# Input laid out transposed as well, norm factor applied at eviction, attention steps moved off VectorE, row work of the end spread

## Chip, cores, metric

One core of a Trainium2 chip runs the whole layer in one launch. The metric is device time in microseconds; the median of three runs of the kernel before is 1140.7 us (1139.41 to 1140.78).

## The reference

One decoder layer on 1024 rows of 1024 columns in float32, with sandwich norms:

```
n    = rmsnorm(x) * pre_mix_gain
proj = n @ w_in                       # u | v | q | k | value | forget logits
a_u, a_v = gelu(proj_u), gelu(proj_v)
a    = a_u * (tril(w_spatial) @ layernorm(a_v) + b_spatial)      # 128-row chunks, 8 groups
logf = log_sigmoid(proj_f + b_f);  c = cumsum(logf)
b    = softmax(q k^T / 8 + c_q - c_k, causal) @ value             # 8 heads of 64, blocks of 128 queries
mix  = [rmsnorm(a) | rmsnorm(b)] @ w_out
h    = x + rmsnorm(mix)
ff   = (silu(n2 @ w_gate) * (n2 @ w_up)) @ w_ffn_out,  n2 = rmsnorm(h)
out  = h + rmsnorm(ff)
```

The norm of x is a factor per row (the reciprocal root of the row's mean square) times a gain per column. A factor per row commutes with the product by w_in; a gain per column does not.

## The kernel before

Every product is made of three products of fp32r halves: `split` (line 113) copies a tile to its high part on ScalarE and subtracts that on VectorE (or GpSimd) for the low part; `mm3` (118) issues high x high, high x low and low x high on TensorE. Loads and stores are all issued on SP's queue, which is in order. The tile framework orders the instructions of each engine by program order and by readiness in its own model, and sets the semaphores; the order on each engine is then fixed.

Stage by stage:

- **Front, value and forget columns ("bv").** For each of 8 row tiles, `norm_load` reads x, `norm_scale` (185 to 190) takes the square sum on ScalarE, the root on VectorE and GpSimd (`rstd`) and multiplies by root and gain on VectorE, and `norm_tr` transposes 8 blocks of 128x128 on TensorE and splits them from PSUM into `nth`/`ntl`, which stay for all projections. Then 48 products of 256 and 264 columns per tile; `split` evicts them into `vs`, and the forget logits go to `fz`. The weights come in 4 pairs of pieces through three `stage` buffers.
- **"av" and "au"**: the same with 512 columns, GELU on ScalarE, layer norm, spatial gating; cumulative sums of the log gates are transposed and stored to `c_d`.
- **Attention**, 4 pairs of heads. `qk_steps` makes q and k transposed, evicting with the factor -1/8 (442 to 449); for pairs 2 to 4 its products are pumped in between the blocks of the pair before. For 64 blocks (head, 128 queries): `prep` on GpSimd, `scores` on TensorE, a fused add-and-minimum on VectorE, the exponential with its sum on ScalarE, a reciprocal of the sum on VectorE (499), `probs` (transposes and splits), `values` every second block, whose result is copied out of PSUM by VectorE (543), and `finish`. `qu_load` (461) brings a unit's queries by four DMAs into one of three buffers. In the last pair w_out is loaded and the first two row tiles are merged.
- **Mix, feed-forward up, feed-forward down**, in Strassen-like forms of seven products. The down projection runs the products 1, 2, 6, 5, 7, 3, 4 with 11 steps each; every step is 12 products of 512 columns, and its operands are loaded and split four steps ahead. In product 4 the row work runs beside: steps 0 to 3 do `square` for both halves of one tile each (multiplication by the gain on GpSimd) and `ffn_tail` (root, two fused multiply-adds on VectorE, two stores); steps 3 to 6 load the h rows of the other four tiles and do their second half. The last four steps are then done tile by tile, and after each, `after` does the first half and the tail of that tile.

Of the kernel before, what the change touches and what calls it, by code (L numbers as in the profile page):

```python
# [36 lines left out]
QUB = 3  # L37
# [12 lines left out]
def hybrid_block(ctx: ExitStack, tc: tile.TileContext, io: dict, out: bass.AP):  # L50
# [40 lines left out]
    rsum = const.tile([P, NT, NH], F32, tag="rsum", name="rsum")  # L91

    an_d = dram.tile([S, AW], F32, tag="an_d", name="an_d")
    bo_d = dram.tile([S, AW], F32, tag="bo_d", name="bo_d")
    c_d = dram.tile([NH * NT, P], F32, tag="c_d", name="c_d")
# [10 lines left out]
    def rstd(ss, n, eps):  # L106
        m = small()
        nc.vector.tensor_scalar(out=m, in0=ss, scalar1=1.0 / n, scalar2=eps, op0=ALU.mult, op1=ALU.add)
        r = small()
        nc.gpsimd.tensor_tensor(out=r, in0=m, in1=mhalf, op=ALU.pow)  # L110
        return r
# [48 lines left out]
    def load_pair(src, width, name, k2, fine=False):  # L160
        raw = stage(f"raw_{name}_{k2}")[:, :2 * width].rearrange("p (a w) -> p a w", a=2)
# [15 lines left out]
    g1 = xp.tile([P, D], F32, tag="g1", name="g1")  # L177
    spare = mixd.rearrange("p t c -> p (t c)")

    def norm_load(t):  # L180
        xt = xp.tile([P, D], F32, tag="x", name=f"x_{t}", bufs=2)
        nc.sync.dma_start(out=xt, in_=x[t * P:(t + 1) * P, :])
        return xt
# [22 lines left out]
    g1_row = spare[0:1, 2 * D:3 * D]  # L206
    nc.sync.dma_start(out=g1_row, in_=io["pre_mix_gain"].rearrange("(o d) -> o d", o=1))
    xts = {0: norm_load(0)}
# [6 lines left out]
    gain = []  # L215
    for b in range(2):
        cs = slice(b * 512, b * 512 + 512)
        o = bank("S", f"g1_{b}")
        nc.tensor.matmul(o, ones[0:1, :], g1_row[:, cs], start=True, stop=True)
        gain.append((cs, o))  # L220
    norm_scale(0, xts[0], gain)
    norm_tr(0, xts[0])
    wvf = [w for k2 in range(KT // 2) for w in load_pair(io["w_bvf"], 520, "bv", k2, True)]
    for cs, o in gain:
        nc.scalar.copy(out=g1[:, cs], in_=o)
    xts[1] = norm_load(1)
    norm_scale(1, xts[1])

# [6 lines left out]
    for t in range(NT):  # L235
        if t + 2 < NT:
            xts[t + 2] = norm_load(t + 2)
        if t + 1 < NT:
            norm_tr(t + 1, xts[t + 1])
        if t + 2 < NT:  # L240
            norm_scale(t + 2, xts[t + 2])
# [7 lines left out]
        for b in range(2):  # L249
# [4 lines left out]
            split(o[:, :256].rearrange("p (h d) -> p h d", d=HD), vs[t][:, hs, :HD], vs[t][:, hs, HD:])  # L254
            if b == 1:
                nc.vector.tensor_tensor(out=fz[:, :, t], in0=o[:, 256:264], in1=bfb, op=ALU.add)
# [26 lines left out]
    def cum_sum():  # L283
# [4 lines left out]
        nc.vector.memset(ct[:, 64:128], 0.0)  # L288
# [6 lines left out]
    def c_rows():  # L295
        o = bank("O", "cT")
        nc.tensor.transpose(o[:, 0:P], ct, ident)
        nc.vector.tensor_copy(out=crow[0:64, :], in_=o[0:64, 0:P])
        nc.sync.dma_start(out=c_d, in_=crow[0:64, :])
# [27 lines left out]
    for t in range(NT):  # L327
# [9 lines left out]
        nc.scalar.activation(v, o, AF.Gelu)  # L337
# [29 lines left out]
    for t in range(NT):  # L367
# [10 lines left out]
        nc.scalar.activation(a, o, AF.Gelu)  # L378
# [31 lines left out]

    cb0 = [cb_tile(f"cb_0_{h}") for h in range(2)]
# [10 lines left out]
    def qk_steps(p):  # L422
# [7 lines left out]
        for which in range(2):  # L430
            tags = ("X", "S") if p == 0 and which == 1 else ("mm", "mm")
            oo = [bank(tags[half], f"qk_{p}_{which}_{half}") for half in range(2)]
            for k in range(KT):
                w = qw[p, which, k // 2]
                for half in range(2):
                    mm3(oo[half], w[:, 0, k % 2, :], w[:, 1, k % 2, :], nth[half][:, k, :], ntl[half][:, k, :],
                        k == 0, k == KT - 1)
                    if k == KT - 1:
                        o = oo[half]
                        ts = slice(half * 512, half * 512 + 512)  # L440
                        if which == 0:
                            qh, ql = [q[:, ts] for q in qp[p]]
                            nc.scalar.activation(qh, o, AF.Copy, scale=-0.125)
                            nc.vector.scalar_tensor_tensor(out=ql, in0=o, scalar=-0.125, in1=qh.bitcast(F32),
                                                           op0=ALU.mult, op1=ALU.subtract)
# [17 lines left out]
    class Block:  # L463
# [15 lines left out]
        def scores(self):  # L479
# [17 lines left out]
            ssum = small()  # L497
            nc.scalar.activation(sm[:, :n], sm[:, :n], AF.Exp, bias=m, scale=-1.0, accum_out=ssum)  # L498
            nc.vector.reciprocal(out=rsum[:, self.i, hh:hh + 1], in_=ssum)
# [16 lines left out]
    class Unit:  # L516
# [14 lines left out]
        def values(self):  # L531
# [11 lines left out]
            nc.vector.tensor_copy(out=self.osb, in_=o[:, :2 * P])  # L543
# [621 lines left out]
    def row_tiles(t):  # L1165
        ht = po.tile([P, D], F32, tag="ht", name=f"ht_{t}", bufs=4)
        nc.sync.dma_start(out=ht, in_=h_d[t * P:(t + 1) * P, :])
        rows[t] = ht, small(2, "sq"), po.tile([P, D], F32, tag="y", name=f"y_{t}", bufs=4)

    def square(t, dh, src, eng):  # L1170
        ht, ss, y = rows[t]
        cs = slice(dh * 512, dh * 512 + 512)
# [4 lines left out]
    def ffn_tail(t):  # L1177
        ht, ss, y = rows[t]
        ts = slice(t * P, (t + 1) * P)
        r = rstd2(ss)  # L1180
        for dh in range(2):
            cs = slice(dh * 512, dh * 512 + 512)
            nc.vector.scalar_tensor_tensor(out=ht[:, cs], in0=y[:, cs], scalar=r, in1=ht[:, cs],
                                           op0=ALU.mult, op1=ALU.add)
            nc.sync.dma_start(out=out[ts, cs], in_=ht[:, cs])
# [6 lines left out]
    def after(p, i):  # L1192
# [16 lines left out]
        else:  # L1209
            square(t1, 0, a, nc.vector)  # L1210
            ffn_tail(t1)
# [82 lines left out]
```

## Time and profile before

| what | value |
|---|---|
| median of three runs | 1140.7 us |
| profiled execution | 1140.83 us |
| its span, first to last instruction | 1138.8 us |
| VectorE, ScalarE, GpSimd busy | 722.2, 515.2, 177.7 us |
| mean granted TensorE clock | 0.993 |
| DMA | 188.29 MB, 165 GB/s on average |

The busy time of TensorE is made of matmuls whose ends are modelled, so that successive ones overlap; the distance between their starts is what one costs. Waits count where TensorE has them; those of other engines cost something only when TensorE stands because of them.

### The profile page before, as it was taken

The page shows a single profiled execution, that of the slowest core. Times are in us where ns is not written, and L with a number is a line of the kernel's source. Part 1 is how long each engine was busy: PE and PEld are TensorE (multiplying, and loading weights), DVE is VectorE, ACT ScalarE, POOL GpSimd, SP SyncE. Part 2 cuts the span into 40 slices and gives each one's busy share as a digit, 9 for nine tenths or more (in the row PEclk, how much of TensorE's full clock was granted, in tenths as well). Part 3 has the DMA queues.
Part 4 walks back from the last instruction along what each step waited for, and adds up shares of the span by engine and source line. Part 5 has one row for each costly group of instructions (what it writes and reads, how often), then busy time and mean ns, then how long its engine had stood idle before and what let it go on. Part 6 is the DMA issues. An engine that isn't in the chain of part 4 may idle for free.

```text
span 1138.8 us, 15652 instructions
## 1 busy us (share of the span) xinstructions
PE 1102.8 (97%) x5421; PEld 915.8 (80%) x5421; DVE 722.2 (63%) x1291; ACT 515.2 (45%) x994; POOL 177.7 (16%) x247
## 2 busy tenths in 40 slices
PE   8999999999999989999999999999999999999995
PEld 6988787888887867877888888888888888888883
DVE  5565423677779656789766576657665454644575
ACT  6343324566568534564333434333333435444461
POOL 3032203334438321000000000000000000200042
PEclk9999999999999999999999999999999999999997
DMA  8120214233355453557665557455744587666665
GB/s 268 58 93 2 74 48 140 77 98 91 87 137 151 133 194 109 177 201 251 230 220 187 185 185 242 165 185 185 243 163 148 211 268 249 196 191 197 193 196 186
DMA packets 86241, 188.29 MB, mean 165 GB/s; under 512 B 9937, under 2 KB 28433, under 8 KB 83474
## 3 DMA queue, kind: packets, MB, share of 16 engines
q1 hardware_dynamic: 86162, 187.29, 50.8%
q8 instruction: 43, 0.70, 0.3%
q14 instruction: 36, 0.29, 0.1%
HBM read 129.28 MB, written 49.58 MB: 157 GB/s over the span
## 4 chain that ended last, share of the span: by engine, by line
PE 54%; DVE 4%; issue 2%; DMA 2%; POOL 1%; ACT 1%; SPq 0%; DVEq 0%; POOLq 0%; ACTq 0%
PE guA L119 7%; PE guA L121 6%; PE guA L120 6%; PE guC L119 3%; PE guC L120 3%; PE guC L121 3%; PE dA L119 3%; PE dA L120 3%; PE dA L121 3%; PE dC L120 3%; PE dC L119 3%; PE dC L121 3%; PE guE L120 2%; PE guE L121 2%; PE guE L119 2%
## 5 line engine op out<-in xcount | busy, mean ns | idle before, releaser
L1175 POOL TENSOR_TENSOR y<-c,gpo 128x512 f32<-128x512 f32 x12 | 20.5, 1731 | 596.3 <-DMA dwr<-ws_d 476.7
L116 DVE TENSOR_TENSOR dal<-dar,dah 128x512 fp32r<-128x512 f32 x77 | 56.4, 734 | 86.6 <-ACT dah L115 84.6
L115 ACT CAST dah<-dar 128x512 fp32r<-128x512 f32 x77 | 48.0, 624 | 102.9 <-PE dC L120 45.8
L120 PE MATMUL dA<-dwl,dah 128*128 128x512 f32 x176 | 69.4, 394 | 3.0 <-DVE dwl L116 3.0
L119 PE MATMUL dA<-dwh,dah 128*128 128x512 f32 x176 | 69.6, 395 | 2.4 <-ACT dah L115 2.4
L121 PE MATMUL dA<-dwh,dal 128*128 128x512 f32 x176 | 69.0, 392 | 0.0
L474 POOL TENSOR_SCALAR sm<-cb,csq 128x128 f32<-128x128 f32 (+3 forms) x64 | 50.6, 791 | 89.9 <-PE pt L509 79.0
L498 ACT ACTIVATE sm<-sm,st 128x128 f32<-128x128 f32 (+3 forms) x64 | 50.0, 781 | 27.7 <-DVE st L494 27.3
L116 DVE TENSOR_TENSOR ptl<-pt,pth 128x512 fp32r<-128x512 f32 (+2 forms) x96 | 51.7, 554 | 10.4 <-ACT pth L115 9.8
L116 DVE TENSOR_TENSOR dwl<-dwr,dwh 128x512 fp32r<-128x512 f32 x77 | 55.4, 720 | 3.7 <-ACT dwh L115 3.6
L115 ACT CAST pth<-pt 128x512 fp32r<-128x512 f32 (+2 forms) x96 | 43.7, 477 | 27.4 <-PE pt L509 27.1
L119 PE MATMUL mx<-woh,mh 128*128 128x512 f32 x128 | 51.6, 403 | 2.6 <-ACT mh L115 2.6
L119 PE MATMUL qk<-nth,qkw 128*128 128x512 f32 x128 | 53.5, 419 | 0.5 <-DVE k L116 0.4
L492 PE MATMUL s<-k,qu 128*128 128x384 f32 (+4 forms) x192 | 51.0, 365 | 1.5 <-DVE st L494 1.4
L116 DVE TENSOR_TENSOR fbc_0l<-ts,fbc_0h 128x1024 fp32r<-128x1024 f32 x22 | 26.9, 1223 | 38.8 <-ACT fbc_0h L115 38.8
L121 PE MATMUL mx<-woh,ml 128*128 128x512 f32 x128 | 50.2, 395 | 1.2 <-DVE ml L116 1.2
L119 PE MATMUL dC<-dwh,dah 128*128 128x512 f32 x132 | 51.3, 389 | 0.0
L120 PE MATMUL dC<-dwl,dah 128*128 128x512 f32 x132 | 51.3, 389 | 0.0
L121 PE MATMUL dC<-dwh,dal 128*128 128x512 f32 x132 | 51.3, 389 | 0.0
L121 PE MATMUL qk<-nth,qkw 128*128 128x512 f32 x128 | 50.5, 395 | 0.1
L120 PE MATMUL qk<-ntl,qkw 128*128 128x512 f32 x128 | 50.4, 394 | 0.0
L120 PE MATMUL mx<-wol,mh 128*128 128x512 f32 x128 | 50.2, 392 | 0.0
(749 smaller groups left out, 3251.3 us busy)
## 6 DMA issues: line engine op xcount, KB each, us to landing
graw<-in_w_gu SPq DMA_DIRECT2D x21, 1024.0 KB, 5.4
wj<-in_w_ffn_out SPq DMA_DIRECT2D x22, 512.0 KB, 4.2
aj<-ff_d SPq DMA_DIRECT2D x22, 512.0 KB, 3.7
dar<-as_d SPq DMA_DIRECT2D x44, 256.0 KB, 3.6
dwr<-ws_d SPq DMA_DIRECT2D x44, 256.0 KB, 3.7
dwr<-in_w_ffn_out SPq DMA_DIRECT2D x33, 256.0 KB, 4.0
dar<-ff_d SPq DMA_DIRECT2D x33, 256.0 KB, 4.4
ff_d<-g SPq DMA_DIRECT2D x22, 256.0 KB, 5.4
```

The lines of the kernel that those rows point to most:

```text
L115: nc.scalar.copy(out=hi, in_=src)
L116: (lo_eng or nc.vector).tensor_tensor(out=lo, in0=src, in1=hi.bitcast(F32), op=ALU.subtract)
L119: nc.tensor.matmul(o, ah, bh, start=first, stop=False, **kw)
L120: nc.tensor.matmul(o, ah, bl, start=False, stop=False, **kw)
L121: nc.tensor.matmul(o, al, bh, start=False, stop=last, **kw)
L474: nc.gpsimd.tensor_scalar(out=sm[:, :n], in0=cbs[hh][:, :n], scalar1=csq[:, hh * NT + i:hh * NT + i + 1], scalar2=1.0, op0=ALU.add, op1=AL ...
L492: nc.tensor.matmul(o[:, :w], qu[:, hl, ts], ks_[hh][:, ks], start=hl == 0, stop=hl == 1)
L498: nc.scalar.activation(sm[:, :n], sm[:, :n], AF.Exp, bias=m, scale=-1.0, accum_out=ssum)
L1175: eng.tensor_tensor(out=y[:, cs], in0=src, in1=gpo[:, cs], op=ALU.mult)
```

## The change

- **Front.** The host array x is also passed as `x_t`, laid out so that a tile's load gives the transposed blocks, and the gain as a column per block. `x_split` multiplies by the gain (a column value spread over 128 rows) and splits, on VectorE and ScalarE. The transposes are gone. `x_norm` still loads x and takes the square sum; the factors go to `rst`. They are applied where products leave PSUM: in `split_scaled`, in the forget logits, as a scale of the GELUs, and for q and k by a multiplication with a row of factors (`rrow`), which is stored with the cumulative sums and loaded back to all partitions. The last pair of weight pieces has a buffer of its own.
- **Attention.** The exponential's sum goes straight into `rsum`; the reciprocal is taken once per row tile in `merge_norm`. The values' bank is copied by ScalarE. The query buffers (`QUB`) fall from 3 to 2.
- **End.** h rows are loaded and a first half done in steps 2 to 5 of product 6, a second tile's half in product 3; product 4 does the rest in steps 2 to 5, and the stores one step later. All multiplications are on VectorE. At the very end the tail of a tile comes behind the first half of the next.

```diff
-QUB = 3
+QUB = 2
...
+        raw = xp.tile([P, 1040], F32, tag="raw3", name="raw_bv_3") if (name, k2) == ("bv", 3) else stage(...)
...
-    def norm_scale(t, xt, gain=None):
-        ss = small()
-        nc.scalar.activation(spare[...], xt, AF.Square, accum_out=ss)
-        r = rstd(ss, D, RMS_EPS)
-        for cs, g in gain or [(slice(0, D), g1)]:
-            nc.vector.scalar_tensor_tensor(out=xt[:, cs], in0=xt[:, cs], scalar=r, in1=g, op0=ALU.mult, op1=ALU.mult)
-    def norm_tr(t, xt):
-        transposed(lambda k: xt[:, k * P:(k + 1) * P], nth[t // 4][:, :, tok(t)], ntl[t // 4][:, :, tok(t)], f"n{t}")
+    def x_columns(t):
+        xt = xp.tile([P, KT, P], F32, tag="xT", name=f"xT_{t}", bufs=2)
+        src = io["x_t"][t].rearrange("p (k t) -> p k t", t=P)
+        for ks in (slice(0, 4), slice(4, 8)) if t == 0 else (slice(0, 8),):
+            nc.sync.dma_start(out=xt[:, ks, :], in_=src[:, ks, :])
+        return xt
+    def x_split(t, xt, parts=1):
+        for i in range(parts):
+            ks = slice(i * KT // parts, (i + 1) * KT // parts)
+            nc.vector.tensor_tensor(out=xt[:, ks, :], in0=xt[:, ks, :],
+                                    in1=g1[:, ks].unsqueeze(2).broadcast_to([P, KT // parts, P]), op=ALU.mult)
+            split(xt[:, ks, :], nth[t // 4][:, ks, tok(t)], ntl[t // 4][:, ks, tok(t)])
+    def x_norm(t):
+        xt = xp.tile([P, D], F32, tag="x", name=f"x_{t}", bufs=2)
         nc.sync.dma_start(out=xt, in_=x[t * P:(t + 1) * P, :])
+        ss = small()
+        nc.scalar.activation(spare[...], xt, AF.Square, accum_out=ss)
+        rstd(ss, D, RMS_EPS, rst[:, t:t + 1])
+    def split_scaled(src, hi, lo, t):
+        r = rst[:, t:t + 1]
+        nc.scalar.activation(hi, src, AF.Copy, scale=r)
+        nc.vector.scalar_tensor_tensor(out=lo, in0=src, scalar=r, in1=hi.bitcast(F32), op0=ALU.mult, op1=ALU.subtract)
...
+    x_split(0, xts[0], 2)
     wvf = [w for k2 in range(KT // 2) for w in load_pair(io["w_bvf"], 520, "bv", k2, True)]
+    xts[1] = x_columns(1)
+    x_split(1, xts[1])
+    x_norm(0)
...
         if t + 2 < NT:
+            xts[t + 2] = x_columns(t + 2)
+            x_split(t + 2, xts[t + 2])
         if t + 1 < NT:
-            norm_tr(t + 1, xts[t + 1])
+            x_norm(t + 1)
...
-        nc.scalar.activation(v, o, AF.Gelu)
+        nc.scalar.activation(v, o, AF.Gelu, scale=rst[:, t:t + 1])
...
+    rrow = at.tile([P, S], F32, tag="rrow", name="rrow")
+    nc.sync.dma_start(out=rrow.rearrange("p (t n) -> p t n", n=P),
+                      in_=c_d[NH * NT:, :].rearrange("t n -> (t n)").partition_broadcast(P))
...
+                        t = stage(f"qkt_{p}_{which}_{half}")[:, :512]
+                        nc.vector.scalar_tensor_tensor(out=t, in0=o, scalar=1.0 if which else -0.125, in1=rrow[:, ts],
+                                                       op0=ALU.mult, op1=ALU.mult)
                         if which == 0:
-                            nc.scalar.activation(qh, o, AF.Copy, scale=-0.125)
-                            nc.vector.scalar_tensor_tensor(out=ql, in0=o, scalar=-0.125, ...)
+                            split(t, *[q[:, ts] for q in qp[p]])
                         else:
-                                split(o[own, :], ks_[2 * p + h][own, ts], ks_[2 * p + h][oth, ts])
+                                split(t[own, :], ks_[2 * p + h][own, ts], ks_[2 * p + h][oth, ts])
...
-            nc.scalar.activation(sm[:, :n], sm[:, :n], AF.Exp, bias=m, scale=-1.0, accum_out=ssum)
-            nc.vector.reciprocal(out=rsum[:, self.i, hh:hh + 1], in_=ssum)
+            nc.scalar.activation(sm[:, :n], sm[:, :n], AF.Exp, bias=m, scale=-1.0,
+                                 accum_out=rsum[:, self.i, hh:hh + 1])
...
-            nc.vector.tensor_copy(out=self.osb, in_=o[:, :2 * P])
+            nc.scalar.copy(out=self.osb, in_=o[:, :2 * P])
...
+        nc.vector.reciprocal(out=rsum[:, t, :], in_=rsum[:, t, :])
...
-    def square(t, dh, src, eng):
+    def square(t, dh, src, y):
...
-        eng.tensor_tensor(out=y[:, cs], in0=src, in1=gpo[:, cs], op=ALU.mult)
+        nc.vector.tensor_tensor(out=y, in0=src, in1=gpo[:, dh * 512:dh * 512 + 512], op=ALU.mult)
...
-            square(t1, 0, a, nc.vector)
-            ffn_tail(t1)
+            square(t1, 0, a, po.tile([P, 512], F32, tag="y", name=f"y_{t1}", bufs=4))
+            if i > 0:
+                ffn_tail(PAIRS[i - 1][1])
+            if i == 3:
+                ffn_tail(t1)
...
-            if p == 4 and j < 4:
-                t0, t1 = PAIRS[j]
-                for dh in range(2):
-                    square(t0, dh, parts[("c11", "c12")[dh], j], nc.gpsimd)
-                ffn_tail(t0)
-            if p == 4 and 3 <= j < 7:
-                t1 = PAIRS[j - 3][1]
-                row_tiles(t1)
-                square(t1, 1, parts["c22", j - 3], nc.gpsimd)
+            if p in (6, 3, 4) and 1 < j < 6:
+                t0, t1 = PAIRS[j - 2]
+                if p == 6:
+                    row_tiles(t0)
+                    square(t0, 0, parts["c11", j - 2], parts["c11", j - 2])
+                elif p == 3:
+                    row_tiles(t1)
+                    square(t1, 1, parts["c22", j - 2], parts["c22", j - 2])
+                else:
+                    square(t0, 1, parts["c12", j - 2], parts["c12", j - 2])
+                    ffn_tail(t0, False)
+            if p == 4 and 2 < j < 7:
+                tail_store(PAIRS[j - 3][0])
```

`ffn_tail(t, store)` leaves its two stores out when `store` is false, and `tail_store` issues them.

## Rows read from the trace of the kernel before

**Rows 1.** The page: busy us, share of the span, instructions.
```profile
PE 1102.8 (97%) x5421; PEld 915.8 (80%) x5421; DVE 722.2 (63%) x1291; ACT 515.2 (45%) x994; POOL 177.7 (16%) x247
```
**Rows 2.** Windows: stretch, then busy us of each engine, clock, DMA share, GB/s.
```profile
10.00:20.00 10.00, 8.88 (x58) 8.44 (x58) 7.00 (x10) 8.37 (x16) 5.40 (x5) 1.00 0.84 267
30.00:60.00 30.00, 30.00 (x254) 30.00 (x253) 13.72 (x29) 11.14 (x24) 1.65 (x3) 1.00 0.13 42
```
**Rows 3.** TensorE in order of time, front: start, length, line; then one tile's transposes.
```profile
9.99 0.58 PE L119 MATMUL bv<-wh_bv,nth 128*128 128x256 f32 x1 [0.46 <-ACT nth L115]
...
33.18 1.03 PE L128 MATMUL tp_n<-ident,x 128*128 128x128 f32 x8
33.97 0.36 PE L119 MATMUL bv<-wh_bv,nth 128*128 128x256 f32 x1
...
65.55 0.40 PE L119 MATMUL av<-wh_av,nth 128*128 128x512 f32 x1
...
L128 PE MATMUL tp_n<-ident,x x64: 270/272/474, 7.6 to 53.9; 128*128 128x128 f32 x64
```
**Rows 4.** ScalarE in order of time: the first square of x.
```profile
4.75 1.06 ACT L187 ACTIVATE mixd<-x 128x1024 f32<-128x1024 f32 x1 [2.69 <-DMA x<-in_x]
```
**Rows 5.** Groups by line and shape: busy us, mean ns, idle before them.
```profile
L190 DVE SCALAR_TENSOR_TENSOR x<-x,st,g 128x1024 f32<-128x1024 f32 x7 | 9.0, 1285 | 4.2 <-POOL st L110 4.2
L499 DVE RECIPROCAL rsum<-st 128x1 f32<-128x1 f32 x64 | 10.3, 161 | 20.3 <-ACT sm L498 20.1
L543 DVE COPY osb<-o 128x256 f32<-128x256 f32 x31 | 12.9, 417 | 6.0 <-PE o L541 6.0
L444 DVE SCALAR_TENSOR_TENSOR ql<-qk,qh 128x512 fp32r<-128x512 f32 x8 | 5.5, 690 | 3.6 <-ACT qh L443 3.6
L443 ACT ACTIVATE qh<-qk 128x512 fp32r<-128x512 f32 x8 | 4.8, 594 | 3.2 <-PE qk L121 3.2
L115 ACT CAST pth<-pt 128x256 fp32r<-128x256 f32 x16 | 5.9, 370 | 4.4 <-PE pt L509 4.4
```
**Rows 6.** Windows of attention: three head pairs; the start of the last.
```profile
200.00:330.00 130.00, 129.01 (x803) 111.62 (x801) 94.81 (x287) 76.64 (x196) 49.98 (x91) 1.00 0.35 95
340.00:350.00 10.00, 7.53 (x47) 5.55 (x45) 9.89 (x28) 7.80 (x20) 9.11 (x10) 1.00 0.59 164
```
**Rows 7.** The query tile: issue and landing of its loads; two blocks' scores.
```profile
L461 SPq DMA_DIRECT2D qu<-qh x64: 461/558/668, 178.4 to 364.9; - x64
DMA to landing us min/median/max: 1.9/2.0/4.9
...
337.25 1.36 PE L492 MATMUL s<-k,qu 128*128 128x384 f32 x4
342.88 0.47 PE L492 MATMUL s<-k,qu 128*128 128x448 f32 x1
```
**Rows 8.** The last stall: SP's waits for stores, TensorE, SP, two windows.
```profile
SPq L1185 <- DVE ht L1183: 24.4, 15, 10.4
...
1113.37 0.42 SPq L1100 DMA_DIRECT2D dar<-ff_d  x1
...
1115.29 0.50 PE L120 MATMUL dA<-dwl,dah 128*128 128x512 f32 x1 [2.97 <-DVE dwl L116]
1118.46 0.80 PE L119 MATMUL dA<-dwh,dah 128*128 128x512 f32 x1 [2.40 <-ACT dah L115]
...
1115.00:1120.00 5.00, 2.32 (x6) 1.52 (x7) 1.52 (x3) 0.71 (x2) 0.00 (x0) 0.58 0.90 313
1120.00:1125.00 5.00, 5.00 (x18) 4.04 (x17) 1.92 (x3) 1.96 (x5) 0.00 (x0) 0.73 0.12 48
```
**Rows 9.** After the last product: TensorE's last, then VectorE's last tile.
```profile
1129.83 0.39 PE L121 MATMUL dA<-dwh,dal 128*128 128x512 f32 x1
...
1132.87 0.68 DVE L1175 TENSOR_TENSOR y<-dA,gpo 128x512 f32<-128x512 f32 x1
...
1134.34 1.41 DVE L1183 SCALAR_TENSOR_TENSOR ht<-y,st,ht 128x512 f32<-128x512 f32 x2 [0.67 <-POOL st L103]
```

More of the change, by code (lines that the diff above doesn't have):

```diff
@@ L160, in load_pair @@
     def load_pair(src, width, name, k2, fine=False):
-        raw = stage(f"raw_{name}_{k2}")[:, :2 * width].rearrange("p (a w) -> p a w", a=2)
+        raw = xp.tile([P, 1040], F32, tag="raw3", name="raw_bv_3") if (name, k2) == ("bv", 3) else stage(f"raw_{name}_{k2}")
+        raw = raw[:, :2 * width].rearrange("p (a w) -> p a w", a=2)
         rows = src[k2 * 2 * P:(k2 + 1) * 2 * P, :].rearrange("(a p) w -> p a w", p=P)
@@ L214, in hybrid_block @@
                             compare_op=ALU.is_equal, fill=0.0)
[L215 to L222, printed above, removed]
+    x_split(0, xts[0], 2)
     wvf = [w for k2 in range(KT // 2) for w in load_pair(io["w_bvf"], 520, "bv", k2, True)]
[L224 to L227, printed above, removed]
+    xts[1] = x_columns(1)
+    x_split(1, xts[1])
+    x_norm(0)
     fz = fp.tile([P, NH, NT], F32, tag="fz", name="fz")
@@ L287, in cum_sum @@
         tot = o[:, 64:128].rearrange("p (h t) -> p h t", t=NT)
[L288 removed]
+        nc.vector.memset(ct[:, 64 + NT:128], 0.0)
+        nc.vector.tensor_copy(out=ct[:, 64:64 + NT], in_=rst)
         nc.vector.memset(car[:, :, 0], 0.0)
@@ L1165, in row_tiles, with tail_store, ffn_tail @@
     def row_tiles(t):
-        ht = po.tile([P, D], F32, tag="ht", name=f"ht_{t}", bufs=4)
+        ht = po.tile([P, D], F32, tag="ht", name=f"ht_{t}", bufs=NT)
         nc.sync.dma_start(out=ht, in_=h_d[t * P:(t + 1) * P, :])
-        rows[t] = ht, small(2, "sq"), po.tile([P, D], F32, tag="y", name=f"y_{t}", bufs=4)
-    def square(t, dh, src, eng):
-        ht, ss, y = rows[t]
-        cs = slice(dh * 512, dh * 512 + 512)
+        rows[t] = ht, po.tile([P, 2], F32, tag="ssq", name=f"ssq_{t}", bufs=NT), {}
+    def square(t, dh, src, y):
+        ht, ss, ys = rows[t]
         s = po.tile([P, 512], F32, tag="junk", name=f"junk_{t}_{dh}", bufs=2)
         nc.scalar.activation(s, src, AF.Square, scale=D ** -0.5, accum_out=ss[:, dh:dh + 1])
-        eng.tensor_tensor(out=y[:, cs], in0=src, in1=gpo[:, cs], op=ALU.mult)
-    def ffn_tail(t):
-        ht, ss, y = rows[t]
-        ts = slice(t * P, (t + 1) * P)
+        nc.vector.tensor_tensor(out=y, in0=src, in1=gpo[:, dh * 512:dh * 512 + 512], op=ALU.mult)
+        ys[dh] = y
+    def tail_store(t):
+        for dh in range(2):
+            cs = slice(dh * 512, dh * 512 + 512)
+            nc.sync.dma_start(out=out[t * P:(t + 1) * P, cs], in_=rows[t][0][:, cs])
+    def ffn_tail(t, store=True):
+        ht, ss, ys = rows[t]
         r = rstd2(ss)
@@ L1182, in ffn_tail @@
             cs = slice(dh * 512, dh * 512 + 512)
-            nc.vector.scalar_tensor_tensor(out=ht[:, cs], in0=y[:, cs], scalar=r, in1=ht[:, cs],
+            nc.vector.scalar_tensor_tensor(out=ht[:, cs], in0=ys[dh], scalar=r, in1=ht[:, cs],
                                            op0=ALU.mult, op1=ALU.add)
-            nc.sync.dma_start(out=out[ts, cs], in_=ht[:, cs])
+        if store:
+            tail_store(t)
     def down_step(o, p, j, i, fresh):
@@ L1220, in hybrid_block @@
         banks = ABANK if p in (1, 6, 7, 4) else cbank
-        if p == 4:
-            for i in range(4):
-                row_tiles(PAIRS[i][0])
         late = range(NJ - 4, NJ) if p == 4 else range(0)
@@ L1269 @@
         "x": a["x"][0],
+        "x_t": a["x"][0].reshape(NT, P, KT, P).transpose(0, 3, 2, 1).reshape(NT, P, KT * P),
+        "pre_mix_gain_t": a["pre_mix_gain"][0].reshape(KT, P).T,
         "w_au": w_in[:, 0:512],
```

36 lines of the change are left out of this document (14 added, 22 removed).

## The prediction

> **What bounds the kernel now.** I read the page first: TensorE is busy for 97% of the span and VectorE for 63% [rows 1]. A count of busy time does not say what a change is worth, so I went on to the windows and to the order of time on TensorE. Only where TensorE starts late, waits, or does something that is no product can time be won. Three places stand out. In the front, products begin at 9.99 and the first projection (the value and forget columns) lasts until 65.55 [rows 3], though TensorE is fully busy from 30 on [rows 2]: late start, waits, and transposes between the tiles. In the middle, attention leaves TensorE 1.0 us idle of 130, and then 2.5 us in the 10 us from 340, where VectorE is busy for 9.9 of 10 [rows 6]. At the end TensorE stops for 2.97 and 2.40 us, runs at a granted clock of 0.58 there, and after its last product at 1129.8 another 9 us pass until the span ends [rows 8, 9].
>
> **Front: the input comes transposed.** Removed per tile of 128 rows are 8 transposes on TensorE. In the rows they start at 33.18 and the next product at 33.97: 0.79 us. From there to 65.55 lie the products of five tiles and three more such groups, so a tile's products take (31.58 - 3 x 0.79) / 5 = 5.84 us, and its period falls from 6.63 to 5.84 [rows 3]. Six tiles in steady state give 6 x 0.79 = 4.7 us. The rest is in the start. Today TensorE waits for: the row to land (4.75), its square sum, the root, the scaling, the transposes, the split [rows 4]. After the change the root is needed only where products leave PSUM, so before the first product stand a multiplication of half a tile (half of the 1.285 us of the scaling, 0.65) and its copy (0.59 for 512 columns, as the scaled copy of the queries [rows 5]): 4.75 + 0.65 + 0.59 = 6.0, and I take 6.5 because the first weight piece is copied by the same ScalarE. The weights come next. With a buffer of its own the last pair of pieces need not wait until one of three stage buffers is free and is issued in one go with the others; the first tile and the weights are 2.7 MB, which at 267 GB/s [rows 2] are 10 us after a first landing about 2 us in, so 12, and with copy and split (1.3) tile 0 ends near 14. Tile 1 needs the next 0.5 MB (2 us more) and 1.3 + 1.1 us of multiplication and copy: it starts near 16 at the worst and 15 at the best. Seven tiles of 5.84 from 15.6 end at 56.5.
>
> Added are 4.2 MB of loads, since the rows are still read for their square sums. From 30 to 60 the engines of the DMA are 13% busy [rows 2], so later tiles hide it: 1 MB per 5.84 us is 180 GB/s. In the first 25 us they do not: the next weights, issued early on SP's queue, can stand ahead of the fourth tile. If all 4.2 MB came on the path, they would cost 15.7 us at 267 GB/s; if none, nothing. I take 1 us, nearest to the row in which they lie beside idle queues. So the stage ends at 57.5 instead of 65.55: **8.0 us**, bounds 3 and 11.
>
> The multiplication by a per-row gain spread over 128 columns is shown by no row; nearest is the scaling at 1.285 us that it replaces [rows 5], and between half and twice that (minus 0.6 to plus 1.3 us per tile) VectorE hides it, busy 13.7 of 30 us in this stage [rows 2]. The square on ScalarE stays. Scaling where products leave PSUM changes a copy into a scaled copy and a subtraction into one with a factor: the scaled pair stands in attention at 0.59 and 0.69 us for 512 columns, and a plain copy of 256 at 0.37 [rows 5], so I cost the difference at nothing, between minus 0.1 and plus 0.1 us per eviction, hidden by TensorE's products; the GELU with a factor goes with it. If the factor itself is late, evictions are, and TensorE stops when the third bank is needed; a row lands one tile ahead, so I give that no term.
>
> *A rule that would give more.* The Trainium skill, page "TensorE: Matmul & The Clock Gate", section "PE-mode transpose", gives about 275 ns for a 128x128 transpose inside a kernel. By it the 64 transposes would be worth an estimated 17.6 us; the rows show 0.79 us for eight, and the measurement decides; what would follow from its figure is rival (e).
>
> **Middle: attention.** Removed from VectorE are 64 reciprocals (0.161 us each, and 20.3 us in which VectorE stood waiting for the exponential's sum before them) and 32 copies of 0.417 us; the copies go to ScalarE at 0.37 each [rows 5]. Added are 16 multiplications of 512 columns out of PSUM by a row of factors, at 0.69, or 11.0 us, after which the splits read SBUF; that is bounded by 0.6 and 0.8. VectorE gets 10.3 + 13.3 - 11.0 = 12.6 us and 20 us of waits back, ScalarE 11.8 more. Almost none of it is on the path: TensorE loses 1.0 us over the first three head pairs [rows 6]. In the last pair VectorE is the bound near 340; eight copies and sixteen reciprocals over 50 us are 1.2 us of each 10, while the last key splits come with 1.4 us of new multiplications just before. I take 0.5 us for the first three pairs and 1.5 for the last: **2.0 us**, bounds -3 (ScalarE stands waiting for the values' bank and holds the casts behind it) and +4. Eight reciprocals of 8 columns before the merges cost 0.16 each and lie long before their use. The chain from the query product to its loads grows by one multiplication, 0.7 us; the key products of 11 us hide it.
>
> The query buffers fall from three to two. A load may then be issued when the scores of the unit before the last are through, three blocks ahead of its use instead of five. Its four transfers take 0.56 us each to issue and land 2.0 later [rows 7]: 2.2 + 2.0 = 4.2 us. The tightest place I found is a block whose scores start at 337.25 and take 1.36, while the unit after next starts at 342.88 [rows 7]: 4.3 us between, so it is just in time. Elsewhere the blocks lie farther apart. I cost it at 0.
>
> **End: row work spread.** The stall comes from SP. Its queue is in order; the stores wait for results that VectorE makes late (24.4 us in 15 waits, one of 10.4), and an activation load that stands behind them is issued only at 1113.37 [rows 8]. TensorE therefore waits until 1118.46, in all 2.97 + 2.40 = 5.4 us. Then the granted clock: 0.58 and 0.73 in the two windows of 5 us [rows 8] are, with 1.2 of 2.4 GHz as the lower level, 4.2 and 2.7 us at half speed, which so end near 1122.7; TensorE works in the last 4.2 of them and loses half, 2.1 us. The change moves the two first quarters of the row work into earlier products, where the queue has no store to wait for, takes GpSimd's multiplications away, and issues each store one step after its result. What VectorE gets in that product is 0.6 + 0.2 + 1.4 us and a wait of 0.7 per tile besides two splits of 0.6, 4.1 in a step of 2.7 us; over four steps it falls 5.6 us behind, against splits that are made four steps (10.9 us) ahead. So I keep 0.7 us of stall and take 6.8 of the 7.5 as won; no stall left would be 7.5, all of it back 0.
>
> After the last product, VectorE today takes the fourth tile's multiplication only at 1132.87, because it is still with the third; the final pair starts at 1134.34 and ends at 1135.75 [rows 9], 5.5 us after the last product. With tiles evenly 2.7 us apart it can multiply 0.75 us after the last product: 0.75 + 0.6 + 0.2 + 0.7 + 1.4 = 3.65. That is 1.8 us. **8.6 us** together, bounds 1 and 9.5.
>
> **Sum.** 8.0 + 2.0 + 8.6 = 18.6 us. The profiled execution took 1140.8 us (span 1138.8 and 2.0 around it), the same as the median of the runs shown. Forecast: 1140.8 - 18.6 = 1122.2 us.
>
> **Rivals.** (a) The front is fed by DMA: 4.2 MB more fall into the stretch where queues are already 84% busy [rows 2], and the fourth and fifth tile wait. Then 3 us of the front remain: 1127.2. For it speaks the full queue up to 30 us, against it the empty one after. (b) The stall at the end survives: VectorE, which now does GpSimd's share, delays splits or stores. For it speaks that it falls 5.6 us behind in my count, against it the lead of four steps. Time: 1122.2 + 6.8 = 1129.0. (c) ScalarE becomes the bound in the last head pair, at the lower bound of the middle term: 1127.2. (d) Slower: the two query buffers. If the loads are late, TensorE stands at the scores of each of about 29 units; it decides against the kernel from 18.6 / 29 = 0.64 us of lateness per unit, and 0.8 gives 1145.4. That needs loads of 6 us or more at most units, so SP must be held behind other waits each time; the margin of 4.3 us at the tightest place speaks for it, the wider ones against. (e) Each transpose costs its whole length, 0.27 us, and not the 0.10 after which the next one starts [rows 3]: 64 x 0.17 = 10.9 us more, 1111.3. Against it stands that the next product starts 0.79 us after the first of eight; for it only that a gap may have been filled by work that was ready anyway. This is what the Trainium skill's page named above would have.
>
> **How the numbers follow.** Forecast case 0.62 (its own range 1117 to 1127), a 0.12, b 0.13, c 0.05, d 0.04, e 0.03, and 0.01 for no change. Two runs that differ by under 0.2% (2.3 us) can't be told apart. Faster: 0.62 + 0.12 + 0.13 + 0.05 + 0.03 = 0.95; same 0.01; slower 0.04. The range must hold both a and b and the upper bounds of the terms: 1113 to 1132.
>
> **What would show it.** Right: no transposes in the first projection, its first product near 6.5 and the next projection's first near 57.5; no wait of TensorE over 1 us after 1090 and a granted clock of 1.00 to its last product; the last pair on VectorE under 4.5 us after it. Wrong: waits for DMA on the third to fifth tile (a), waits of the down projection for splits (b), TensorE waiting for ScalarE's copies near 330 (c), or for the query tile at the scores (d).

## The result, and the profile after

The changed kernel takes 1132.59 us (median of 4 runs, 1131.49 to 1133.70) against 1140.74 for the kernel before beside it: a ratio of 0.993 [0.9913, 0.9947] (95% interval in brackets, here and below), 8.1 us faster. The forecast was 18.6 us, and 1132.6 lies 0.6 above the top of the range. The same kernel again, later, gave 1134.22 us and 0.995 [0.9931, 0.9969] (e5 below): less than half of the forecast either way.

Cut at the first product of each stage, the profiled executions stand as follows (us). Pairs 1-3 run from the first product of q and k to the first scores of the last pair, the last pair from there to the scores of its last block, the tail from the end of the last product. The last column gives where TensorE was granted 1.2 instead of 2.4 GHz, ahead of the end of the down projection; each such stretch is 3.4 us long (6.8 where "x2" stands) and costs at most half of that.

| kernel | front | av, au | pairs 1-3 | last pair | mix | up | down | tail | half clock at |
|---|---|---|---|---|---|---|---|---|---|
| before | 65.55 | 100.35 | 175.10 | 44.64 | 102.67 | 424.37 | 217.54 | 8.56 | 123, 1116 x2 |
| after | 59.81 | 100.35 | 176.75 | 49.05 | 103.57 | 425.00 | 210.39 | 7.04 | 18, 117, 339, 407 |
| e5 (after again) | 60.01 | 99.08 | 177.02 | 49.20 | 102.54 | 424.54 | 210.41 | 7.01 | 406 |
| after - before | -5.74 | 0.00 | +1.65 | +4.41 | +0.90 | +0.63 | -7.15 | -1.52 | |

The sum is -6.82, the difference of the spans (1132.0 and 1138.8). The front and the end give 14.4 us; attention takes 6.1 of them back, and mix and up 1.5. Each row of the table is one execution. The kernel after has a half-clock stretch in its last pair (339), worth up to 1.7 us; e5 has none there and the same length, so the lengths of that pair are compared with e5 where it matters.

The page, busy us with share of the span and instructions; then windows with busy us of PE, PEld, DVE, ACT, POOL, the granted clock, DMA share, GB/s.
```profile
PE 1095.6 (97%) x5353; PEld 910.2 (80%) x5353; DVE 719.4 (64%) x1225; ACT 527.9 (47%) x1017; POOL 162.6 (14%) x235
```
```profile
10.00:20.00 10.00, 8.07 (x53) 7.64 (x53) 7.91 (x6) 4.47 (x9) 5.93 (x4) 0.92 0.67 262
30.00:60.00 30.00, 30.00 (x250) 30.00 (x249) 14.85 (x30) 15.06 (x27) 3.75 (x6) 1.00 0.54 180
200.00:330.00 130.00, 128.02 (x790) 109.80 (x789) 88.54 (x236) 83.28 (x214) 52.68 (x92) 1.00 0.34 91
...
1115.00:1120.00 5.00, 4.76 (x21) 3.60 (x22) 2.73 (x6) 1.18 (x3) 0.55 (x1) 1.00 0.03 11
1120.00:1125.00 5.00, 4.92 (x22) 3.75 (x20) 3.55 (x8) 0.89 (x4) 1.09 (x2) 1.00 0.57 210
```
Against [rows 2, 6, 8]: the loads of the front now lie beside full TensorE work (30 to 60: DMA at 0.54 instead of 0.13, TensorE still 30.00 of 30). VectorE is down over three head pairs (88.5 of 130 instead of 94.8), and yet TensorE is idle 2.0 us there instead of 1.0. The last windows are whole again, at clock 1.00.

The front in order of time: start, length, engine, line, operation [idle before, releaser]; TensorE, then VectorE.
```profile
7.35 0.80 PE L120 MATMUL bv<-wh_bv,nth 128*128 128x256 f32 x2 [7.35 <-ACT wh_bv L116]
...
16.67 0.39 PE L120 MATMUL bv<-wh_bv,nth 128*128 128x256 f32 x1 [1.18 <-ACT nth L116]
...
17.93 0.39 PE L122 MATMUL bv<-wh_bv,ntl 128*128 128x256 f32 x1 [0.76 <-DVE st L109]
...
59.81 0.39 PE L120 MATMUL av<-wh_av,nth 128*128 128x512 f32 x1
...
4.83 1.29 DVE L194 TENSOR_TENSOR xT<-xT,g 128x512 f32<-128x512 f32 x2 [3.83 <-DMA g<-in_pre_mix_gain_t]
...
13.22 2.32 DVE L194 TENSOR_TENSOR xT<-xT,g 128x1024 f32<-128x1024 f32 x1
...
17.86 1.22 DVE L194 TENSOR_TENSOR xT<-xT,g 128x1024 f32<-128x1024 f32 x1
```
Where [rows 3] have their transposes, products now follow products. Two things are late in the start: the first multiplication waits until 4.83 for the gain column, a small load issued behind the first tile, and the second tile's multiplication takes 2.32 us instead of 1.22, after the weights' splits on VectorE. e8 below tries both.

The end: TensorE's only wait after 1090 (us, times, longest), then the last tile in order of time, TensorE's last product and VectorE.
```profile
PE dA L121 <- DVE dwl L117: 0.2, 1, 0.2
```
```profile
1124.53 0.39 PE L122 MATMUL dA<-dwh,dal 128*128 128x512 f32 x1
...
1125.45 0.75 DVE L1198 SCALAR_TENSOR_TENSOR ht<-c,st,ht 128x512 f32<-128x512 f32 x1
1126.11 0.68 DVE L1185 TENSOR_TENSOR y<-dA,gpo 128x512 f32<-128x512 f32 x1
...
1127.64 0.75 DVE L1198 SCALAR_TENSOR_TENSOR ht<-y,st,ht 128x512 f32<-128x512 f32 x1 [0.73 <-POOL st L104]
```
The stall of [rows 8] is gone, and the last fused pair starts 3.1 us after the start of the last product where [rows 9] have 4.5.

### The profile page after: what moved, and what is told of

Same layout as the page of the kernel before. It is cut to its first block, busy times and chain, and to the rows that moved or that the text cites. A ratio compares the mean times of both kernels' runs of the same rounds, so it can differ in the third digit from the quotient of the medians.

```text
span 1132.0 us, 15484 instructions
## 1 busy us (share of the span) xinstructions
PE 1095.6 (97%) x5353; PEld 910.2 (80%) x5353; DVE 719.4 (64%) x1225; ACT 527.9 (47%) x1017; POOL 162.6 (14%) x235
## 4 chain that ended last, share of the span: by engine, by line
PE 81%; DVE 6%; DMA 4%; ACT 3%; issue 3%; POOL 2%; SPq 1%; POOLq 0%; DVEq 0%; ACTq 0%
PE guA L120 7%; PE guA L121 7%; PE guA L122 7%; PE guC L121 3%; PE guC L122 3%; PE guC L120 3%; PE dA L121 3%; PE dA L122 3%; PE dA L120 3%; PE dC L122 3%; PE dC L120 3%; PE dC L121 3%; PE qk L122 2%; PE qk L121 2%; PE qk L120 2%
## 5 line engine op out<-in xcount | busy, mean ns | idle before, releaser
L104 POOL TENSOR_TENSOR st<-st,mhalf 128x1 f32<-128x1 f32 x17 | 12.1, 715 | 663.4 <-DVE st L102 663.4
L117 DVE TENSOR_TENSOR dal<-dar,dah 128x512 fp32r<-128x512 f32 x77 | 53.2, 692 | 82.6 <-ACT dah L116 82.6
L507 ACT ACTIVATE sm<-sm,st 128x128 f32<-128x128 f32 (+3 forms) x64 | 49.9, 780 | 17.4 <-DVE st L504 16.6
L117 DVE TENSOR_TENSOR dwl<-dwr,dwh 128x512 fp32r<-128x512 f32 x77 | 52.7, 685 | 2.3 <-ACT dwh L116 2.3
```

The lines of the kernel that those rows point to most:

```text
L117: (lo_eng or nc.vector).tensor_tensor(out=lo, in0=src, in1=hi.bitcast(F32), op=ALU.subtract)
```

## The experiments

Theories, as the expectations name them: A, the copy of the values' bank costs in the last pair because it now stands in ScalarE's queue; B, two query buffers cost; C, the multiplication by the row of factors costs VectorE time that TensorE waits for.

**Copy back on VectorE (e1_osb_vector)**
```diff
-            nc.scalar.copy(out=self.osb, in_=o[:, :2 * P])
+            nc.vector.tensor_copy(out=self.osb, in_=o[:, :2 * P])
```


> The changed kernel with one edit undone: the values' bank is copied out of PSUM by VectorE again, not by ScalarE. Theory A (ScalarE's queue: the copy stands behind casts of w_out and exponentials, and TensorE waits for it at the transposes of the result; 0.57, 0.83 and some hidden waits in the trace): the last block's scores start near 383.5 instead of 385.96, the median falls by 2 to 4 us, to about 1129.5. Theory B (two query buffers): no change, 1132 to 1133. Theory C (the multiplication by the factor row at the eviction of q and k): no change. Theory D (the end of attention hangs on something that the change did not touch, so the gain of the front is lost whatever is undone): no change.

Measured: 1130.02 us, 0.9902 [0.9882, 0.9922]; last pair 46.21, pairs 1-3 177.25. This one line of the change costs 2.6 us by medians (4.2 against e5, where the intervals are apart; those of e1 and of the first measurement overlap), and it costs them in the last pair: 46.21 against 49.20 in e5, with no half-clock stretch in either.

**The copy alone, on the kernel before (e6_before_scalar_copy)**: the reverse edit of line 543.

> The kernel before with one edit of the change alone: ScalarE copies the values' bank out of PSUM. Theory A (ScalarE's queue): block 48 to block 63 takes 1.5 us or more longer than 44.64, and the median rises by 1 to 3 us to 1142 to 1144. Theory E (the copy hurts only together with the later changes, for instance because the reciprocals no longer pace VectorE): within 0.7 us of the kernel before in that stretch, and no change of the median.

Measured: 1142.89 us, 1.0018 [1.0007, 1.0028] (10 runs): slower alone, as theory A has it. The last pair takes 49.44 instead of 44.64, with no half-clock stretch in either; pairs 1-3 gain 0.53. The whole run loses 1.8 us by medians, less than the last pair does: in the profiles 0.5 came back in pairs 1-3, 0.6 in the down projection, and 1.25 since this execution had no half-clock stretch near 120. TensorE's waits in the last pair of this kernel (us in total, times, longest), then ScalarE and TensorE in order of time:
```profile
PE pt L509 <- DVE ptl L116: 2.7, 3, 1.8
PE ot L550 <- DVE ptl L116: 2.0, 2, 1.6
PE ot L550 <- ACT osb L543: 1.9, 2, 1.4
```
```profile
346.83 0.62 ACT L115 CAST woh<-woraw 128x512 fp32r<-128x512 f32 x1 [1.26 <-DMA woraw<-in_w_out]
347.36 0.37 ACT L543 COPY osb<-o 128x256 f32<-128x256 f32 x1
...
347.78 0.44 PE L550 MATMUL ot<-ident,osb 128*128 128x128 f32 x2 [1.41 <-ACT osb L543]
```
The copy stands behind a cast that waits 1.26 us for w_out, and TensorE waits 1.41 us for the copy. The changed kernel shows the same, and the copy behind an exponential too:
```profile
356.60 0.62 ACT L116 CAST woh<-woraw 128x512 fp32r<-128x512 f32 x1 [1.11 <-DMA woraw<-in_w_out]
357.12 0.61 ACT L586 CAST woh<-woraw 128x512 fp32r<-128x512 f32 x1
357.64 0.37 ACT L552 COPY osb<-o 128x256 f32<-128x256 f32 x1
...
358.07 0.44 PE L559 MATMUL ot<-ident,osb 128*128 128x128 f32 x2 [0.57 <-ACT osb L552]
...
369.26 0.83 ACT L507 ACTIVATE sm<-sm,st 128x640 f32<-128x640 f32 x1 [1.03 <-DVE st L504]
...
370.50 0.44 PE L559 MATMUL ot<-ident,osb 128*128 128x128 f32 x2 [0.83 <-ACT osb L552]
```
These direct waits are 1.4 us of the changed kernel's last pair. The experiments charge the copy with 3 to 5; the rest is in waits for VectorE's splits, whose share due to the copy no run separates.

**Eviction without the row of factors (e3_plain_evict)**: q and k leave PSUM as before (442 to 449 of the kernel before).

> The changed kernel with q and k evicted as before, without the multiplication by the factor row (so the norm factor is left out of q and k; the row is loaded but not used). Theory C (the sixteen multiplications and the longer chain cost the middle its time): 2 to 4 us faster, near 1129.5, with the loss in the first three head pairs (2.2 us) mostly gone. Theories A, B and D: within 1 us of 1132.6.

**The same, and three query buffers (e2_plain_three_query)**: besides, `rrow` isn't loaded and `QUB = 3`.

> As the kernel with the plain eviction, but the factor row is not loaded either and its space holds a third query buffer, as before the change (the norm factor is left out of q and k). Theory B (two query buffers make the scores wait): 2 us or more faster than the kernel with the plain eviction. Theories A, C and D: within 1 us of that kernel.

These two and e4 leave the norm factor out of q and k: they price a step, and are no replacement for it.

Measured: e3 1131.38 us, 0.9919 [0.9895, 0.9943], pairs 1-3 174.89; e2 1131.10 us, 0.9914 [0.9895, 0.9933], pairs 1-3 174.92. B is refuted: the third buffer changes neither. (Beside the row of factors there is no room for it, so it was not tried on the changed kernel itself.) C holds for pairs 1-3: 174.9 without the row, 176.75 and 177.02 with it. The time alone does not show it: e3 is 1.2 us below the first measurement and 2.8 below e5, and its interval overlaps with both. Both kernels still lose in the last pair, where the copy stayed on ScalarE (47.68 in e3; e2 has two half-clock stretches in it). But e3's 47.68 is also 1.5 below e5's 49.20, so the row costs in the last pair too. One place of it, TensorE at the scores of the pair's second block, in e5 (on VectorE a key split stands ahead of the fused add that TensorE waits for), then in e3:
```profile
336.08 0.88 DVE L117 TENSOR_TENSOR k<-qkt,k 64x512 fp32r<-64x512 f32 x1
...
337.67 0.50 PE L502 MATMUL s<-k,qu 128*128 128x256 f32 x2 [1.12 <-DVE st L504]
```
```profile
335.10 0.50 PE L502 MATMUL s<-k,qu 128*128 128x256 f32 x2 [0.67 <-DVE st L504]
```

**Attention as before, front and end changed (e4_attention_before)**: e2 with VectorE's copy and the reciprocal of each block.

> The changed front and end with the whole attention as before: copy on VectorE, a reciprocal per block, three query buffers, plain eviction (the norm factor is left out of q and k). Theories A to C together: the gains of front and end stand alone, 1140.7 - 5.7 - 8.6 = 1126.4, and the last block's scores start near 381. Theory D: the last scores still start near 386 and the time is 1131 to 1133.

Measured: 1128.17 us, 0.989 [0.987, 0.9911]; pairs 1-3 175.28 and last pair 45.01, as before the change. By medians the whole attention change costs 4.4 us (against 1132.59; 6.1 against e5). Theory D is out: the last scores start at 380.74, not near 386.

**The changed kernel again (e5_same_again)**: no edit.

> The changed kernel once more, unchanged, as a control. If the loss of the last head pair belongs to the kernel, block 48 to block 63 takes 47 to 49 us again (49.05 in the first profile, 44.64 in the kernel before) and the median is 1132 to 1133. If it was an accident of one execution (a stretch at the lower clock that may or may not fall there), it takes near 45 and the median is near 1129.

Measured: 1134.22 us, 0.995 [0.9931, 0.9969]. In its profile the last pair takes 49.20 with no half-clock stretch in it, so the clock is not why that pair is long.

**End alone (e12_end_alone)**: the kernel before with the change's end.

> The kernel before with the row work of the end spread as in the change, and nothing else. Theory of the forecast (SP's queue behind late stores, and the late last tile): the down projection takes 210.4 us instead of 217.5, 7.0 us pass from its last product to the end instead of 8.6, and the time falls by 8.6 us to about 1132. Theory H (the end is faster only because the rest of the changed kernel shifted what the queue holds): less than 4 us.

Measured: 1131.92 us, 0.993 [0.9915, 0.9946], down 210.39 and tail 7.16, with no half-clock stretch from 1090 to its last product. Theory H is out. TensorE's one wait after 1090:
```profile
PE dA L120 <- DVE dwl L116: 0.2, 1, 0.2
```
A third of the change has the ratio of the whole, 0.993: what the front wins is what attention loses. From e12 to e4 the front adds 5.6 us, each set against the kernel before beside it (7.25 and 12.88 faster); the bare medians are 3.75 apart, but the kernel before took 1139.17 beside e12 and 1141.05 beside e4.

**All low parts of q and k on GpSimd (e7_low_gpsimd)**: e1, and
```diff
-                            split(t, *[q[:, ts] for q in qp[p]])
+                            split(t, *[q[:, ts] for q in qp[p]], nc.gpsimd)
...
-                                split(t[own, :], ks_[2 * p + h][own, ts], ks_[2 * p + h][oth, ts])
+                                split(t[own, :], ks_[2 * p + h][own, ts], ks_[2 * p + h][oth, ts], nc.gpsimd)
```


> The changed kernel with the copy on VectorE, and the low halves of q and k made on GpSimd instead of VectorE, which the factor row's multiplication makes possible since they are read from SBUF now. Theory C' (what the factor row costs is VectorE's time): the stretch from the first query product to block 48 falls from 177.3 to 175 or less, and the time by 2 us against the kernel with the copy on VectorE alone (1130.0). Theory C'' (it is the longer chain or the GpSimd work that counts): no gain, or a loss because GpSimd's preparation of the blocks comes late.

Measured: 1132.51 us, 0.9928 [0.9908, 0.9949]: 2.5 us above e1, with overlapping intervals. Pairs 1-3 fall to 175.88 with a half-clock stretch in them, but the last pair takes 51.02 with one in it; at most 1.7 us of that is the stretch, so it is at least 3 us longer than e1's 46.21. There is no gain, as theory C'' has it, but the gain in pairs 1-3 that C' expects is not excluded.

**Front: gain column first, second tile in halves (e8_front_halves)**: e1, with the gain column's load issued ahead of `x_columns(0)`, and
```diff
-    x_split(1, xts[1])
+    x_split(1, xts[1], 2)
```


> The changed kernel with the copy on VectorE, the gain column loaded ahead of x, and the second tile multiplied and split in two halves like the first. Theory F (the front misses its forecast because the gain column lands late, and because the second tile's one large multiplication lets TensorE stand, after which it runs at the lower clock): first product near 6.8 instead of 7.4, first product of the second projection near 57, no stretch at half clock before 60, time about 1128.5. Theory G (the front is fed by DMA, so the order on VectorE does not matter): the second projection starts at 58.5 to 60 as before.

Measured: 1129.13 us, 0.99 [0.9881, 0.9918]; first product 6.64, front 57.68. The four kernels with this edit have fronts of 57.68 to 58.42, the seven with the change's own 57.94 to 60.10; their first products start at 6.64 to 7.68 and at 7.00 to 7.45. The ranges overlap, so theory F is not settled: an early start shows in this execution, and no gain beyond the scatter. The ratio is not told apart from e1's.

**Copy on ScalarE in the first three pairs only (e9_copy_split)**: e8 with
```diff
+            (nc.scalar.copy if self.p < NPAIR - 1 else nc.vector.tensor_copy)(out=self.osb, in_=o[:, :2 * P])
```


> The kernel with the two halves in the front, but the values' bank is copied by ScalarE in the first three head pairs and by VectorE in the last. Theory A (the copy hurts where ScalarE also casts w_out, so in the last pair alone): block 48 to 63 takes about 46 to 48 as with the copy on VectorE everywhere, and the first three pairs take 176 to 177.4; time 1128 to 1129. Theory A' (the copy on ScalarE hurts wherever it stands): the first three pairs lose against 177.4, or the last pair is above 48.

Measured: 1129.95 us, 0.992 [0.9908, 0.9932]; pairs 1-3 176.82 instead of e8's 177.39. No gain that the times show. The last pair takes 48.96; that is above the 48 that A' names, but with 6.8 us at half clock in it (up to 3.4 us of time; e8's 48.00 has 6.8 too) it decides nothing.

**Low parts on GpSimd for the second and third pair only (e10_low_two_pairs)**: e8 with e7's edit as `nc.gpsimd if p in (1, 2) else nc.vector`.

> The kernel with the two halves in the front and the copy on VectorE, with the low halves of q and k made on GpSimd for the second and third head pair alone (their eviction lies between the blocks of the pair before, where GpSimd has room). Theory C' (the factor row costs the first three pairs VectorE's time): first query product to block 48 falls from 177.4 to about 175.5, the last pair stays at 46 to 48, time 1126.5 to 1128. Theory C'' (the longer chain counts): 177 or more, no gain.

Measured: 1126.59 us, 0.9882 [0.9868, 0.9897]: the lowest median and ratio of all, 12.6 us below the kernel before beside it (1139.17), and with an interval below the changed kernel's. Against e8, from which it differs by this one edit, the ratios are not told apart, but pairs 1-3 are: 174.57 instead of 177.39, with no half-clock stretch in either. The last pair takes 48.10, with 6.8 us at half clock in it. TensorE's waits in pairs 1-3 (us in total, times, longest), of the kernel before, of after, of e8 and of this one:
```profile
PE pt L509 <- DVE ptl L116: 0.7, 2, 0.5
PE qk L119 <- DVE k L116: 0.4, 1, 0.4
PE pt L509 <- ACT sm L498: 0.3, 1, 0.3
PE s L492 <- DVE st L494: 0.2, 1, 0.2
```
```profile
PE pt L518 <- DVE ptl L117: 1.7, 3, 0.9
PE s L502 <- DVE st L504: 1.1, 3, 0.4
PE ot L559 <- ACT osb L552: 0.2, 1, 0.2
```
```profile
PE s L502 <- DVE st L504: 1.2, 3, 0.5
PE pt L518 <- ACT sm L507: 0.8, 3, 0.3
PE ot L559 <- DVE osb L552: 0.7, 1, 0.7
PE s L502 <- DVE k L117: 0.2, 1, 0.2
```
```profile
PE s L503 <- DVE st L505: 1.2, 3, 0.5
PE o L548 <- ACT pth L116: 0.2, 1, 0.2
```
They add up to 1.6, 3.0, 2.9 and 1.4 us, beside 175.10, 176.75, 177.39 and 174.57: the two with the row's multiplications and all their splits on VectorE wait longer. What is waited for depends on what stands behind the row's work. In the changed kernel it is the split of the probabilities (ptl); in e8, where the copy is on VectorE, it is that copy (osb) and exponentials (sm), and these are the waits that e10 removes. The sums cover half of the 2.8 us between e8 and e10; where the rest goes, the list does not show. The longest case of the changed kernel:
```profile
226.67 1.05 DVE L117 TENSOR_TENSOR k<-qkt,k 64x512 fp32r<-64x512 f32 x1
...
228.34 1.40 DVE L117 TENSOR_TENSOR k<-qkt,k 64x512 fp32r<-64x512 f32 x2
229.78 1.02 DVE L117 TENSOR_TENSOR ptl<-pt,pth 128x512 fp32r<-128x512 f32 x2
...
230.62 0.52 PE L518 MATMUL pt<-ident,sm 128*128 128x128 f32 x3 [0.88 <-DVE ptl L117]
```
The key halves' splits, which come right after their multiplication, stand ahead of it on VectorE.

**e10 with the copy on ScalarE in the first three pairs (e11_mix_low)**: the lines of e9 and e10 together.

> The best version so far (two halves in the front, low halves of q and k on GpSimd for the second and third pair), with the copy on ScalarE in the first three head pairs and on VectorE in the last. Theory A: harmless there, first query product to block 48 takes 174.0 to 174.8, time 1126 to 1127. Theory A' (the copy on ScalarE costs wherever it stands, and its place in the first three pairs was only hidden behind VectorE's load, which is gone now): 176 or more, time 1128 or more.

Measured: 1128.68 us, 0.99 [0.9881, 0.9918]; pairs 1-3 175.82 instead of 174.57, and waits of TensorE for ScalarE's copy come back (0.5 us once). In pairs 1-3 the copy on ScalarE gained 0.53 us in e6 and 0.57 in e9 and loses 1.25 here; whether it is a gain or a cost there is not settled.

## Why the prediction was wrong, by its own steps

**Front, 8.0 forecast, 5.7 measured (within its bounds).** The steady period was right: products of the third to the eighth tile start 5.79 us apart (5.84 forecast), so the eight transposes of a tile were worth about the 0.79 us of [rows 3]: before, tiles with a group of them start 6.65 apart, 0.86 more. Rival (e) is out, since the whole length of eight (270 ns each in [rows 3]) would have been 2.2 us. The Trainium skill (page "TensorE: Matmul & The Clock Gate", section "PE-mode transpose") gives about 275 ns for one; an estimate by it is 2.2 us for a group too, and the trace does not agree. The start was too hopeful: the first product at 7.35 (6.5), the second tile at 16.67 (15.6), and 2.6 us more lost up to the third tile, at a wait of TensorE (0.76) and a half-clock stretch at 18.4 (up to 1.7). The control has full clock there and a front of 60.01, since its second tile starts only at 17.62; so the stretch alone isn't the reason, and why the start varies stays open. The 1 us for DMA was not needed: the later tiles' loads are hidden (windows above), and TensorE waits for no load. Rival (a) is out.

**Middle, 2.0 us gain forecast, 6.1 us loss measured: the step that failed.** The prediction had "I take 0.5 us for the first three pairs and 1.5 for the last: **2.0 us**, bounds -3"; the trace gives -1.65 and -4.41, beyond the lower bound, and the control, with no half-clock stretch in either, -1.92 and -4.56. No row stood behind the 0.5 and the 1.5: "Almost none of it is on the path" was taken from TensorE's small idle time, which limits what can be won there and not what can be lost. It held two errors, each shown by an undo.
- *The copy in the last pair* was priced as 0.37 us of an engine with time to spare. Its engine's queue was not looked at: just there ScalarE holds the w_out casts, which wait for their loads, and exponentials. In executions without a half-clock stretch in the last pair the copy costs 44.64 to 49.44 alone (e6), 45.01 to 47.68 beside the change's reciprocal and two buffers (e3) and 46.21 to 49.20 on top of it all (e1, e5): 2.7 to 4.8 us. Rival (c) had the engine and the place at a chance of 0.05, and the bound it rested on had the order reversed ("ScalarE stands waiting for the values' bank and holds the casts behind it"): it is the casts that hold the copy, as the rows at 356.60 to 358.07 show.
- *The factor row* was counted on VectorE's total, as 11.0 us against 23.6 removed. The size was right (x16 at 688 ns), the conclusion not: VectorE's total fell, but these instructions come in bursts with the splits that follow them, and what TensorE waits for stands behind them. Undone in e3, it gave back 2.1 us in pairs 1-3 and 1.5 in the last pair (against e5, one execution each). Besides, some of the splits, which read SBUF now, became longer: the medians are 687 and 692 ns for k and ql, the longest 1171 and 1551. Groups of attention after: busy us, mean ns, idle before.
```profile
L117 DVE TENSOR_TENSOR k<-qkt,k 64x512 fp32r<-64x512 f32 x16 | 12.2, 761 | 1.5 <-ACT k L116 1.0
L452 DVE SCALAR_TENSOR_TENSOR qkt<-qk,rrow 128x512 f32<-128x512 f32 x16 | 11.0, 688 | 2.1 <-PE qk L122 2.0
...
L117 DVE TENSOR_TENSOR ql<-qkt,qh 128x512 fp32r<-128x512 f32 x8 | 6.4, 807 | 1.3 <-ACT qh L116 1.3
```
[rows 5] have a mean of 690 for the last of these. With e10's placement the same multiplications cost pairs 1-3 nothing (174.57, where before took 175.10), so it is the multiplications and splits together on VectorE that cost, not the multiplications as such.

The query buffers at 0 were right (B refuted, rival (d) out). The copies taken off VectorE brought no gain that a time shows (in pairs 1-3, 0.53 us in e6 and 0.57 in e9, about the 0.5 taken, and a loss in e11); no run moves the reciprocals alone.

**End, 8.6 forecast, 8.7 measured** (-7.15 - 1.52), and confirmed alone by e12. Its parts: 7.15 for stall and clock, where 6.8 were taken with 0.7 us of stall left and 7.5 without any; 0.2 us was left. The tail won 1.5 instead of 1.8: the last multiplication starts 1.2 us after the last product has ended (1124.92), not 0.75, since VectorE is with the third tile's fused pair until then (row at 1125.45). Rival (b) is out.

**Sum.** 8.0 + 2.0 + 8.6 became 5.7 - 6.1 + 8.7 = 8.3, and mix and up took 1.5 of it away in this execution: the 6.8 of the spans (8.1 by medians; the profiled execution was the slowest of its four). The control's mix and up are 0.0 us longer than before's together, so those 1.5 are no cost of the change. The range held each rival alone; two terms short at once, the front by 2.3 and the middle by 8.1, left it by 0.6. That the miss is so small owes nothing to the middle: its loss exceeded the bound twice over, and the front and the end, forecast at 16.6 and measured at 14.4, carried the gain.

**Left open.** How the copy's 3 to 5 us divide between its own lateness and what that does to the order on VectorE; and, in e6, why it costs 4.8 on the kernel before and about 3 beside the rest of the change. The last pair of e1 is still 1.2 to 1.6 us longer than in e4 and before; that is the size of what the row costs between e3 and e5 (1.5), so the row is the likely reason, but no run with the copy on VectorE leaves the row alone out.

## What to carry to other kernels

An instruction moved to an idler engine is priced by what stands ahead of it in that engine's queue at the place where it is needed, above all a cast that waits for a load, and not by the engine's busy share. A row of work added to an engine with slack overall is on the path if it comes in a burst ahead of something another engine waits for; put it on the engine that has a gap at that time, pair by pair (e10), not everywhere (e7). Test the parts of a change one by one: here a third of it had nearly the whole gain (e12), and one line cost 3 us in the last pair.

## What the runs showed of the hardware

Stretches at a granted 1.2 GHz of 3.4 us fall differently in executions of one kernel. Windows of two stretches, after and then the same kernel again (columns as above):
```profile
335.00:340.00 5.00, 3.48 (x20) 2.37 (x19) 4.87 (x13) 4.43 (x11) 1.91 (x3) 0.92 0.94 334
405.00:410.00 5.00, 3.76 (x11) 2.66 (x11) 3.29 (x5) 1.74 (x4) 0.38 (x2) 0.75 0.21 83
```
```profile
335.00:340.00 5.00, 3.10 (x24) 2.47 (x22) 4.91 (x12) 4.38 (x12) 2.37 (x3) 1.00 0.97 327
405.00:410.00 5.00, 3.75 (x11) 2.77 (x10) 3.12 (x6) 2.29 (x5) 0.55 (x1) 0.66 0.34 110
```
TensorE is partly idle in all four; near 339 one execution lost clock and the other did not. A stage is therefore compared above between executions that have no such stretch in it, or the stretch is named.

A multiplication of 1024 columns on VectorE took 2.32 us at 13.22, while GpSimd split weights from 9.41 to 14.45, and 1.22 at 17.86; the same in halves (e8) took 2.39 at 13.00. That GpSimd is the reason is not shown: no run takes its splits away.
